# Hybrid retention and attention layer: p.v in fp32 in the two column halves of TensorE, row maxima of two heads in its two row halves

## The chip, the cores and the metric

The kernel runs on one core of a Trainium2 chip. Its time is the device time of one execution in microseconds; the figure for the kernel before is the median of three runs. The profile is of one execution, so every duration below is of that one.

TensorE is called PE in the views, VectorE DVE, ScalarE ACT and GpSimd POOL.

## What is computed

One layer, applied to two sequences with the same weights: a sequence of 1024 tokens (the prompt, names ending in `p`) and one of 512 tokens (the sample, names ending in `s`). Only the attention half of the layer is touched:

```python
def blocked_gqa(q, k, v):            # 8 query heads, 2 key/value heads, head size 64
    ...
    def one_block(qi):               # 128 queries
        sc = jnp.einsum('bqkgd,bskd->bkgqs', qi, k).astype(jnp.float32) * scale
        p = jax.nn.softmax(sc, axis=-1).astype(v.dtype)
        return jnp.einsum('bkgqs,bskd->bqkgd', p, v)
...
mixed = jnp.concatenate([ret_out * jax.nn.silu(rg), att_out * jax.nn.silu(ag)], axis=-1) @ w_out
return x + gate[:, None, :] * mixed
```

All of it is fp32. The kernel uses two ways of multiplying fp32 numbers on TensorE: operands of type fp32r, which it splits into a high and a low part to add several products, each matmul being one record in the trace; or operands left fp32, unsplit, where one matmul is two records in the trace.

## The kernel before

The sample goes first (its attention is swept at about 207 to 335 us), the prompt second (about 669 to 981 us). Attention is swept in tiles of 128 queries: four tiles for the sample, eight for the prompt (`nt`). Heads 0 to 3 share key/value head v=0, heads 4 to 7 share v=1.

Per tile, the steps and their lines are these. `nat_prep` transposes the eight heads of q, high part stacked on low part (L841), and ACT copies them to `Q1T` (L844). `nat_head`, once a head, multiplies them with the keys into a wide PSUM buffer (L854; two matmuls of 512 columns in the prompt, one in the sample), and DVE takes the negated row maximum (L856). `fill_q2`, `mid` and `mid_t` put q and the maximum side by side (POOL's copy in `pcopy`, L142; DVE's L865), transpose that (L872) and copy it to `Q2T` of 65 rows (L874), so that the score matmul of the low key part also subtracts the maximum. `st_unit`, eight times a tile in the prompt, four in the sample, makes the transposed scores of four heads against 256 keys (two matmuls L897, two L909), ACT takes the exponential (L912), ACT casts the high part `ph` (L138, in `split`), DVE subtracts for the low part `pl` (L139), and POOL adds p into an accumulator (L921, L924). `pv_unit` multiplies with v, four matmuls of 512 columns (L939, L940); v's high and low parts are side by side in the stationary operand, so the two halves of the result are added at the end (L950 on ACT, L951 on DVE). `row_sums` sums POOL's accumulator over keys with an fp32 matmul with ones, one for v=0 and one for v=1, which write to the two column halves (L958). `normalise` takes Ln and Exp of that (L963, L964), multiplies with the gate (L969) and with o (L970). `out_step` multiplies the finished tile with the output weights (`mm3`, L148 to L150, tile name `py`), 48 matmuls of 512 columns a tile. They are the work that fills the spaces of the next tile.

The order is written out in rounds, one round a unit (`per_` is nt + 1 rounds a tile); in each round the steps stand by a priority number, and a scheduler then places the instructions:

```python
at_round(hb + u, 1, lambda t=t, h=u * hp + h, n=n: nat_head(t, h, ...))
at_round(b + u, 3, lambda t=t, u=u: st_unit(t, u))
at_round(b + u + 1, 4, lambda t=t, u=u: pv_unit(t, u))
at_round(b + nt, 4.5, lambda t=t: row_sums(t))
```

`hb` is one tile ahead of `b`, so the maxima of the next tile are made while the scores of this one are. PSUM has eight banks, shared by `wide` buffers of two banks and `bank` buffers of one: two wide and four single in the sample's attention, three and two in the prompt's.

## Time and profile before

| | |
|---|---|
| time, median of 3 runs (lowest, highest) | 988.04 us (985.65, 988.46) |
| the profiled execution: span | 985.3 us |
| instructions | 15952 |
| PE busy | 938.8 us, 95% of the span |
| DVE busy | 626.1 us, 64% |
| POOL busy | 507.7 us, 52% |
| ACT busy | 414.3 us, 42% |

Of the profiled execution the span is what is known: 985.3 us, 2.7 us under the median of the three runs, which are timed without a profile. Busy is the time in which an engine's records run. A matmul's record is longer than the time to the next matmul's start, since matmuls overlap; so the price of a matmul is read from one start to the next one's.

### The profile page before, as it was taken

Reading aid. Unit: us, or ns where it says so; the run is one execution under the profiler, and the core shown is the slowest. Engines: PE = TensorE matmul, PEld = TensorE weight load, DVE = VectorE, ACT = ScalarE, POOL = GpSimd, SP = SyncE. Lnnn points to the kernel's source line nnn. Section 1 sums busy time; section 2 is a strip of 40 time slices with the busy share of each in tenths; the row PEclk is TensorE's granted clock in tenths of the full one; section 3 lists DMA queues with packets and bytes.
Section 4 is the critical chain, followed back from the end, with each engine's and each line's share of the span. In section 5 each row is a group of like instructions: output and inputs, shape, how many; then the busy total and the mean of one; then the engine's idle time right before and its main releaser. Section 6 shows DMA issues by size and latency. Waiting matters only on the chain. (4 is left out here: it accounts for less than half of the span.)

```text
span 985.3 us, 15952 instructions
## 1 busy us (share of the span) xinstructions
PE 938.8 (95%) x6249; PEld 813.9 (83%) x6249; DVE 626.1 (64%) x1039; ACT 414.3 (42%) x656; POOL 507.7 (52%) x404
## 2 busy tenths in 40 slices
PE   4889998999999999999999999999979999999998
PEld 3779898987676799999999988999847776776776
DVE  2474556667886683534435243457988878978975
ACT  4252233353646652122321322241465655655562
POOL 4243544474647663122223012255899779777882
PEclk9999998999999999999999999999999999999999
DMA  9964876321911711111111112100071110111011
GB/s 274 275 191 144 269 225 218 87 78 57 382 67 44 239 50 47 41 43 44 44 35 28 26 43 70 47 7 12 1 296 68 43 44 1 44 43 45 20 43 44
DMA packets 95687, 93.02 MB, mean 94 GB/s; under 512 B 23502, under 2 KB 84858, under 8 KB 92540
## 3 DMA queue, kind: packets, MB, share of 16 engines
q1 hardware_dynamic: 92876, 77.85, 25.8%
q0 software_dynamic: 2736, 14.16, 3.6%
q8 instruction: 49, 0.80, 0.3%
q14 instruction: 26, 0.21, 0.1%
HBM read 77.30 MB, written 14.68 MB: 93 GB/s over the span
## 5 line engine op out<-in xcount | busy, mean ns | idle before, releaser
L924 POOL TENSOR_TENSOR qp<-qp,pp 128x512 f32<-128x512 f32 x96 | 159.5, 1661 | 21.3 <-ACT pp L912 15.3
L139 DVE TENSOR_TENSOR plp<-pp,php 128x1024 fp32r<-128x1024 f32 x64 | 93.6, 1464 | 19.8 <-ACT php L138 19.7
L912 ACT ACTIVATE pp<-pTp 128x1024 f32<-128x1024 f32 x64 | 65.6, 1025 | 76.8 <-PE pTp L909 40.7
L856 DVE TENSOR_REDUCE nmp<-pnp 128x1 f32<-128x1024 f32 x64 | 77.3, 1212 | 11.4 <-PE pnp L854 11.4
L138 ACT CAST php<-pp 128x1024 fp32r<-128x1024 f32 x64 | 67.2, 1051 | 16.2 <-PE pop L939 14.9
L148 PE MATMUL pvgp<-wvgp,hhp 128*128 128x256 f32 x224 | 65.1, 291 | 0.0
L148 PE MATMUL pqkp<-wqkp,hhp 128*128 128x256 f32 x224 | 64.7, 289 | 0.0
L149 PE MATMUL pvgp<-wvgp,hhp 128*128 128x256 f32 x224 | 64.4, 288 | 0.0
L150 PE MATMUL pvgp<-wvgp,hlp 128*128 128x256 f32 x224 | 63.9, 285 | 0.0
L150 PE MATMUL pqkp<-wqkp,hlp 128*128 128x256 f32 x224 | 63.7, 284 | 0.0
L149 PE MATMUL pqkp<-wqkp,hhp 128*128 128x256 f32 x224 | 63.4, 283 | 0.0
L940 PE MATMUL pop<-plp,VVp 128*128 128x512 f32 x128 | 52.1, 407 | 5.7 <-DVE plp L139 5.6
L148 PE MATMUL pyp<-wo,Mhp 128*128 128x512 f32 (+1 forms) x136 | 52.8, 389 | 1.2 <-DVE op L951 0.7
L150 PE MATMUL pyp<-wo,Mlp 128*128 128x512 f32 (+1 forms) x136 | 51.6, 382 | 0.5 <-DVE Mlp L139 0.5
L149 PE MATMUL pyp<-wo,Mhp 128*128 128x512 f32 (+1 forms) x136 | 51.9, 382 | 0.0
L639 POOL TENSOR_TENSOR sp<-rt1p,rt2p 128x512 f32<-128x512 f32 x16 | 22.5, 1405 | 56.4 <-DVE rt2p L636 56.4
L939 PE MATMUL pop<-php,VVp 128*128 128x512 f32 x128 | 51.0, 398 | 0.3 <-ACT php L138 0.3
L124 POOL TENSOR_SCALAR m_retp<-ssp 128x4 f32<-128x4 f32 x8 | 1.6, 195 | 89.6 <-DVE ssp L745 89.4
L897 PE MATMUL pTp<-Q1Tp,kkp 128*128 128x512 f32 x128 | 41.4, 404 | 3.6 <-ACT pp L912 2.9
L148 PEld LDWEIGHTS pqkp<-wqkp,hhp 128*128 128x128 f32 x224 | 43.0, 192 | 0.0
L149 PEld LDWEIGHTS pqkp<-wqkp,hhp 128*128 128x128 f32 x224 | 43.0, 192 | 0.0
L150 PEld LDWEIGHTS pqkp<-wqkp,hlp 128*128 128x128 f32 x224 | 42.9, 192 | 0.0
(465 smaller groups left out, 3120.7 us busy)
## 6 DMA issues: line engine op xcount, KB each, us to landing
wo<-wod SPq DMA_DIRECT2D x16, 1024.0 KB, 5.8
wa<-in_w_ada_dram SPq DMA_DIRECT2D x16, 512.0 KB, 6.4
wod<-woz POOLq DMA_DIRECT2D x8, 1024.0 KB, 6.0
gr<-in_w_ada_dram SPq DMA_DIRECT2D x16, 256.0 KB, 4.8
xn<-in_x_prompt_dram SPq DMA_DIRECT2D x8, 512.0 KB
xrp<-in_x_prompt_dram SPq DMA_DIRECT2D x8, 512.0 KB, 3.4
out_dram<-xrp POOLq DMA_DIRECT2D x7, 512.0 KB, 3.0
xs<-in_x_sample_dram SPq DMA_DIRECT2D x4, 512.0 KB, 6.1
```

The source lines that it names most:

```text
L138: hi_eng(hi, src)
L139: lo_eng.tensor_tensor(lo, src, hi.bitcast(F32), op=ALU.subtract)
L148: T.matmul(out, lh, rh, start=first, stop=False)
L149: T.matmul(out, lh, rl, start=False, stop=False)
L150: T.matmul(out, ll, rh, start=False, stop=last)
L639: G.tensor_tensor(qk, t1, t2, op=ALU.add)
L856: V.tensor_reduce(nm[:, h : h + 1], pn[:, :ntok], AX.X, ALU.max, negate=True)
L897: T.matmul(pT[:, i * 512 : (i + 1) * 512], kk[v][:, kb], st8[t]["Q1T"][:, hs, :].rearrange("p h q -> p (h q)"), start=True, stop=False)
L912: S.activation(p, pT, AF.Exp)
L924: G.tensor_tensor(acc, acc, p[:, i * 512 : (i + 1) * 512], op=ALU.add)
L939: T.matmul(po, lv, ph[:, c], start=(kb == 0), stop=False)
L940: T.matmul(po, lv, pl[:, c], start=False, stop=(kb == nt - 1))
```

## The change

Four things are changed.

1. p and v are multiplied in fp32. p is not split (no cast, no subtraction), v is kept as one fp32 copy. The matmul of a head group has 64 output rows, so v=0 is put into column half 0 and v=1 into column half 1 of the array, one after the other: `pv_pair`, four matmuls for 256 keys of both v, which all wait for the exponential of the second of two units. Units therefore alternate between v=0 and v=1. The result `po` is in one bank for the whole tile and is read by `normalise` directly.
2. The row maxima are taken from the high part of q and k alone, with 64 contracted rows a head. Two heads are put into the two row halves of the array: `nat_pairs`, for two units two wide buffers, each with two heads against 512 keys. In the prompt the two maxima of a head (512 keys each) are then combined by DVE.
3. The eight maxima of a tile are transposed once (a matmul of 128 columns into 8 rows), and two DVE multiplications with a part of the identity matrix spread them over rows 64 to 71 of `Q2T`; `k2` has eight rows of ones for them. Rows 0 to 63 are copied by DVE from `Q1T`. POOL's copy and the second set of transposes fall away.
4. The two row sum matmuls stand together, behind POOL's last addition, and their buffer is a wide one. The sample's attention also has three wide buffers and two single ones.

```diff
-                kv["k2"] = [kvp.tile([65, ntok], F32R, name=f"k2{tg}{v}") for v in range(2)]
-                kv["V"] = kvp.tile([P, nt, 2, 2, DH], F32R, name=f"VV{tg}")
+                kv["k2"] = [kvp.tile([72, ntok], F32R, name=f"k2{tg}{v}") for v in range(2)]
+                kv["V"] = kvp.tile([P, nt, 2, DH], F32, name=f"VV{tg}")
...
-                        for v in range(2):
-                            src = pj[:, :, P + v * DH : P + (v + 1) * DH]
-                            S.copy(VV[:, gs_, v, v, :], src)
-                            V.tensor_tensor(VV[:, gs_, v, 1 - v, :], src, VV[:, gs_, v, v, :].bitcast(F32), op=ALU.subtract)
+                        S.copy(VV[:, gs_, :, :], pj[:, :, P : 2 * P].rearrange("p t (v d) -> p t v d", v=2))
...
-            nwide.append(2 if first else 3)
+            nwide.append(3)
...
+                Qg = Q1.rearrange("p (g h) a d -> p g (h a) d", h=2)
+                split(*((S.copy, V) if t == order[0] else (pcopy, G)), Qg[:, :, 0::3, :], Qg[:, :, 1:3, :], qv)
...
+            def fill_q2(t):
                 d = st8[t]
-                Q1T, nm = d["Q1T"], d["nm"]
-                v = h // 4
-                pn = (bank if nt == 4 else wide)(f"pn{tg}{t}{h}")
-                for n in range(ng):
-                    c = slice(n * 512, (n + 1) * 512)
-                    T.matmul(pn[:, c], Q1T[:, h, :], kk[v][:, c], start=True, stop=True)
-                with tc.issue_after(prev["mid"].ins) if "mid" in prev else ExitStack():
-                    V.tensor_reduce(nm[:, h : h + 1], pn[:, :ntok], AX.X, ALU.max, negate=True)
-
-            def fill_q2(t, v):
-                b0 = (t % 2) * 512 + v * 256
-                Q2 = st8[t]["Q2", v] = ate.tile([P, 4, 65], F32R, tag=f"Q2{v}", name=f"Q2{tg}{t}{v}", bufs=1)
-                pcopy(Q2[:, :, 0:DH], qs[t // 2][:, b0 : b0 + 256].rearrange("p (h d) -> p h d", d=DH))
-
-            def mid(t, v):
+                Q1T = d["Q1T"]
+                Q2T = d["Q2T"] = pools["q2"].tile([72, QH, P], F32R, tag="Q2T", name=f"Q2T{tg}{t}", bufs=Q2BUFS[r])
+                for i in range(2):
+                    V.tensor_copy(Q2T[0:DH, i::2, :], Q1T[i * DH : (i + 1) * DH, i::2, :])
...
+            def nat_pairs(t, units, prev):
                 d = st8[t]
-                d["mid"] = V.tensor_copy(d["Q2", v][:, :, DH], d["nm"][:, 4 * v : 4 * v + 4])
-
-            def mid_t(t, v):
+                Q1T = d["Q1T"]
+                pns = [wide(f"pn{tg}{t}{u}") for u in units]
+                with tc.high_priority():
+                    for j, u in enumerate(units):
+                        pr, n = u // ng, u % ng
+                        for i in range(2):
+                            rows = slice(i * DH, (i + 1) * DH)
+                            m = T.matmul(pns[j][:, i * 512 : (i + 1) * 512], Q1T[rows, 2 * pr + i, :],
+                                         kk[pr // 2][rows, n * 512 : (n + 1) * 512], start=True, stop=True)
+                for j, u in enumerate(units):
+                    pr, n = u // ng, u % ng
+                    out = (d["nm"] if ng == 1 else d["nmh"][:, n, :])[:, 2 * pr : 2 * pr + 2]
+                    with tc.issue_after(prev["mid"].ins) if "mid" in prev else ExitStack():
+                        V.tensor_reduce(out, pns[j].rearrange("p (i k) -> p i k", i=2), AX.X, ALU.max, negate=True)
...
+            def mid(t):
                 d = st8[t]
-                Q2 = d["Q2", v]
-                pq = wide(f"pq2{tg}{t}{v}")[:, 0:512]
-                for h in range(4):
-                    T.transpose(pq[0:65, h * P : (h + 1) * P].bitcast(F32R), Q2[:, h, :], identr)
-                q2 = d["Q2T", v] = pools["q2"].tile([65, 512], F32R, tag=f"Q2T{v}", name=f"Q2T{tg}{t}{v}", bufs=1)
-                V.tensor_copy(q2, pq[0:65, :])
+                if ng > 1:
+                    V.tensor_tensor(d["nm"], d["nmh"][:, 0, :], d["nmh"][:, 1, :], op=ALU.min)
+                pm = wide(f"pnm{tg}{t}")[0:QH, 0:P]
+                T.transpose(pm.bitcast(F32R), d["nm"], identr)
+                for v in range(2):
+                    hs = slice(4 * v, 4 * v + 4)
+                    d["mid"] = V.tensor_tensor(d["Q2T"][DH:72, hs, :], pm.unsqueeze(1).broadcast_to([QH, 4, P]),
+                                               ident[0:QH, hs].unsqueeze(2).broadcast_to([QH, 4, P]), op=ALU.mult)
...
-                split(S.copy, V, ph, pl, p)
-                d[u] = (ph, pl)
+                p = d["p", u] = pools["at"].tile([P, 1024], F32, tag="p", name=f"p{tg}{t}{u}", bufs=PBUFS[r])
+                d["exp", u] = S.activation(p, pT, AF.Exp)
...
+            def pv_pair(t, kp):
                 d = st8[t]
-                v, kp = u // (nt // 2), u % (nt // 2)
-                ph, pl = d.pop(u)
+                ps = [d.pop(("p", 2 * kp + v)) for v in range(2)]
                 if kp == 0:
-                    d["po"] = bank(f"po{tg}{t}{v}")
-                if u == 0:
-                    d["o"] = pools["q2"].tile([P, 512], F32, tag="o", name=f"o{tg}{t}", bufs=3 if first else 1)
-                po, o = d["po"], d["o"]
-                for i in range(2):
-                    kb = 2 * kp + i
-                    c = slice(i * 512, (i + 1) * 512)
-                    lv = VV[:, kb, v, :, :].rearrange("p a d -> p (a d)")
-                    T.matmul(po, lv, ph[:, c], start=(kb == 0), stop=False)
-                    T.matmul(po, lv, pl[:, c], start=False, stop=(kb == nt - 1))
-                if t in pesum:
-                    if u == 0:
-                        d["L"] = bank(f"pL{tg}{t}")
-                    for i, z in enumerate((ph, pl)):
-                        for j in range(2):
-                            T.matmul(d["L"], vones[v], z[:, j * 512 : (j + 1) * 512],
-                                     start=(u == 0 and i + j == 0), stop=(u == nt - 1 and i + j == 2))
-                if kp == nt // 2 - 1:
-                    mn = slice(v * DH, (v + 1) * DH)
-                    S.copy(o[mn, :], po[(1 - v) * DH : (2 - v) * DH, :])
-                    V.tensor_tensor(o[mn, :], po[mn, :], o[mn, :], op=ALU.add)
+                    d["po"] = bank(f"po{tg}{t}")
+                with tc.high_priority():
+                  for i in range(2):
+                    for v in range(2):
+                        m = T.matmul(d["po"][v * DH : (v + 1) * DH, :], VV[:, 2 * kp + i, v, :], ps[v][:, i * 512 : (i + 1) * 512],
+                                     start=(kp + i == 0), stop=(2 * kp + i == nt - 1))
+                        if v == 0:
+                            tc.add_manual_dep(m.ins, d["exp", 2 * kp + 1].ins.name, SYNC, reason="both column halves at once")
 
             def row_sums(t):
-                if t in pesum:
-                    return
-                pl = st8[t]["L"] = bank(f"pL{tg}{t}") if nt == 4 else wide(f"pL{tg}{t}")[:, 0:512]
+                d = st8[t]
+                pl = d["L"] = wide(f"pL{tg}{t}")[:, 0:512]
                 for v in range(2):
-                    T.matmul(pl[v * DH : (v + 1) * DH, :], ones, qs[tps[0]][:, v * 512 : (v + 1) * 512], start=True, stop=True)
+                    m = T.matmul(pl[v * DH : (v + 1) * DH, :], ones, qs[tps[0]][:, v * 512 : (v + 1) * 512], start=True, stop=True)
+                    if v == 0:
+                        tc.add_manual_dep(m.ins, d["sum", 1].ins.name, SYNC, reason="both halves at once")
...
+                lg = d["o"] = pools["q2"].tile([P, 512], F32, tag="o", name=f"o{tg}{t}", bufs=3 if first else 1)
                 with tc.issue_after(acts["ln"].ins):
...
-                V.tensor_tensor(o, o, pl, op=ALU.mult)
+                    jc = slice(jj * 256, (jj + 1) * 256)
+                    V.tensor_tensor(lg[:, jc].rearrange("p (j q) -> p j q", j=2), pl[:, jc].rearrange("p (j q) -> p j q", j=2),
+                                    gv, op=ALU.mult)
+                V.tensor_tensor(lg, po, lg, op=ALU.mult)
...
+                at_round(hb + per_ - 2 if n == 0 else b - 2, 7.5, lambda t=t: fill_q2(t))
+                at_round(hb + per_ - 1 if n == 0 else b - 1, 7, lambda t=t: mid(t))
                 for u in range(nt):
-                    for h in range(hp):
+                    if u % 2 == 0:
                         at_round(hb + u, 1,
-                                 lambda t=t, h=u * hp + h, n=n: nat_head(t, h, st8[order[0]] if n == 1 else {}))
+                                 lambda t=t, u=u, n=n: nat_pairs(t, (u, u + 1), st8[order[0]] if n == 1 else {}))
                     at_round(b + u, 3, lambda t=t, u=u: st_unit(t, u))
-                    at_round(b + u + 1, 4, lambda t=t, u=u: pv_unit(t, u))
+                    if u % 2:
+                        at_round(b + u + 1, 4, lambda t=t, u=u: pv_pair(t, u // 2))
```

On PE at the border of two tiles of the prompt (where one tile's row sums and the next tile's first scores stand) the kernel before has these rows; `pLp` is the row sums' buffer, `pnp` a maximum's, `pTp` a score's, `pop` p.v's, `pq1p` that of q's transposes:

```order
L841 MATMUL pq1p_9151<-identr,Q1p_9148 128x128 x3
L150 MATMUL pyp_9079<-wo_8052,Mlp_8890 128x512
L939 MATMUL pop_9065<-php_9114,VVp 128x512 [waits Activation_49]
L958 MATMUL pLp_9144<-qp_7145,zo 64x512 [waits Pool_49]
L940 MATMUL pop_9065<-plp_9115,VVp 128x512 [waits DVE_49]
L939 MATMUL pop_9065<-php_9114,VVp 128x512
L940 MATMUL pop_9065<-plp_9115,VVp 128x512
L854 MATMUL pnp_9174<-kkp_6773,Q1Tp_9160 128x512 [waits Activation_49]
L854 MATMUL pnp_9174<-kkp_6773,Q1Tp_9160 128x512
L897 MATMUL pTp_9187<-Q1Tp_8881,kkp_6773 128x512 [waits PE_49]
L897 MATMUL pTp_9187<-Q1Tp_8881,kkp_6773 128x512
L909 MATMUL pTp_9187<-Q2Tp_9063,k2p_6775 128x512 x2
```

After the change the same place reads as follows (line numbers are those of the changed kernel: L940 the row sums, L876 the transposed maxima, L840 q's transposes, L863 the maxima, L901 and L912 the scores):

```order
L940 MATMUL pLp_8166<-qp_6926,zo 64x512 [waits PE_49,Pool_49]
L940 MATMUL pLp_8166<-qp_6926,zo 64x512
L876 MATMUL pnmp_8170<-identr,nmp_7973 8x128 [waits PE_49]
L840 MATMUL pq1p_8177<-identr,Q1p_8174 128x128 [waits PE_49]
L840 MATMUL pq1p_8177<-identr,Q1p_8174 128x128 x7
L863 MATMUL pnp_8202<-kkp_6566,Q1Tp_8186 128x512 [waits DVE_49,Activation_49]
L863 MATMUL pnp_8202<-kkp_6566,Q1Tp_8186 128x512
L863 MATMUL pnp_8203<-kkp_6566,Q1Tp_8186 128x512 [waits PE_49]
L863 MATMUL pnp_8203<-kkp_6566,Q1Tp_8186 128x512
L901 MATMUL pTp_8219<-Q1Tp_7971,kkp_6566 128x512 [waits DVE_49,Activation_49]
L901 MATMUL pTp_8219<-Q1Tp_7971,kkp_6566 128x512
L912 MATMUL pTp_8219<-Q2Tp_8147,k2p_6568 128x512 x2
```

The two row sums now stand in a row behind POOL, q's transposes have moved behind them, and nothing of `py` or of p.v stands between the row sums and the next tile's scores.

On PE in the middle of a tile the kernel before has p.v in fours, in the full array:

```order
L150 MATMUL pyp_9079<-wo_8052,Mlp_8890 128x512
L940 MATMUL pop_9065<-plp_9053,VVp 128x512 [waits DVE_49]
L939 MATMUL pop_9065<-php_9052,VVp 128x512
L940 MATMUL pop_9065<-plp_9053,VVp 128x512
L939 MATMUL pop_9065<-php_9090,VVp 128x512 [waits Activation_49]
L148 MATMUL pyp_9079<-wo_8052,Mhp_8889 128x512
```

After it, four matmuls with 64 output rows stand behind one wait for ACT:

```order
L151 MATMUL pyp_8118<-wo_7766,Mlp_7982 128x512
L149 MATMUL pyp_8118<-wo_7766,Mhp_7981 128x512
L150 MATMUL pyp_8118<-wo_7766,Mhp_7981 128x512
L151 MATMUL pyp_8118<-wo_7766,Mlp_7982 128x512
L931 MATMUL pop_8049<-pp_8127,VVp 64x512 [waits Activation_49]
L931 MATMUL pop_8049<-pp_8143,VVp 64x512
L931 MATMUL pop_8049<-pp_8127,VVp 64x512
L931 MATMUL pop_8049<-pp_8143,VVp 64x512
L149 MATMUL pyp_8229<-wo_7765,Mhp_8196 128x512 [waits DVE_49]
```

The number of matmuls for a unit of 256 keys and four heads goes from four to two, and their four stand together.

On ACT at the same border the kernel before has:

```order
L138 CAST php_9114<-pp_9112 128x1024 [waits PE_49,Activation_49]
L138 CAST Mhp_9447<-mTp 128x512 [waits PE_49]
L844 CAST Q1Tp_9160<-pq1p_9151 128x1024 [waits PE_49]
L963 ACTIVATE pLp_9144<-pLp_9144 128x512 [waits PE_49]
L950 COPY op_8944<-pop_9065 64x512 [waits PE_49]
L964 ACTIVATE pLp_9144<-pLp_9144 128x512 [waits Activation_49]
L912 ACTIVATE pp_9192<-pTp_9187 128x1024 [waits DVE_49,PE_49,Pool_49]
L138 CAST php_9194<-pp_9192 128x1024 [waits Activation_49]
```

After the change (L949 and L950 are Ln and Exp of the row sums, L843 the copy of `Q1T`, L915 the exponential of the scores):

```order
L915 ACTIVATE pp_8143<-pTp_8138 128x1024 [waits PE_49,Pool_49]
L139 CAST Mhp_8411<-mTp 128x512 [waits DVE_49,PE_49]
L949 ACTIVATE pLp_8166<-pLp_8166 128x512 [waits DVE_49,PE_49,Activation_49]
L843 CAST Q1Tp_8186<-pq1p_8177 128x1024 [waits PE_49]
L950 ACTIVATE pLp_8166<-pLp_8166 128x512 [waits Activation_49]
L915 ACTIVATE pp_8224<-pTp_8219 128x1024 [waits PE_49,Pool_49]
L139 CAST Mhp_8196<-op_8190 128x512 [waits DVE_49]
L915 ACTIVATE pp_8238<-pTp_8233 128x1024 [waits PE_49,Pool_49]
```

The casts `php` are gone, and the copy of `Q1T` has moved from ahead of Ln to between Ln and Exp.

## Rows read from the trace of the kernel before

**Rows 1.** The page, part 1: busy time of an engine, its share of the span, instructions.
```profile
PE 938.8 (95%) x6249; PEld 813.9 (83%) x6249; DVE 626.1 (64%) x1039; ACT 414.3 (42%) x656; POOL 507.7 (52%) x404
```

**Rows 2.** Windows of the two attention stages: length, busy us of each engine, granted clock.
```profile
247.00:335.00 88.00, 86.06 (x376) 62.98 (x375) 63.80 (x84) 50.34 (x70) 52.17 (x48) 1.00 0.47 175
696.00:981.00 285.00, 272.00 (x1213) 203.88 (x1212) 235.55 (x251) 163.67 (x184) 228.49 (x148) 0.99 0.15 58
```

**Rows 3.** Source line L958: minimum/median/maximum ns, first and last start.
```profile
L958 PE MATMUL pLp<-qp,zo x32: 592/642/1112, 720.5 to 969.1; 128*64 128x512 f32 x32
```

**Rows 4.** Timeline of PE: start us, length us, line, operation, names, how many.
```profile
748.11 0.41 PE L872 MATMUL pq2p<-identr,Q2p 128*65 128x128 f32 x4
748.35 0.44 PE L940 MATMUL pop<-plp,VVp 128*128 128x512 f32 x1
748.63 0.39 PE L939 MATMUL pop<-php,VVp 128*128 128x512 f32 x1
748.86 0.40 PE L940 MATMUL pop<-plp,VVp 128*128 128x512 f32 x1
```

**Rows 5.** Timeline of PE around one L958.
```profile
765.83 0.40 PE L940 MATMUL pop<-plp,VVp 128*128 128x512 f32 x1
766.15 1.07 PE L958 MATMUL pLp<-qp,zo 128*64 128x512 f32 x2
767.15 0.50 PE L149 MATMUL pyp<-wo,Mhp 128*128 128x512 f32 x1
767.49 0.39 PE L150 MATMUL pyp<-wo,Mlp 128*128 128x512 f32 x1
```

**Rows 6.** Timeline of PE, ACT and DVE around the last two L958.
```profile
968.60 1.08 PE L958 MATMUL pLp<-qp,zo 128*64 128x512 f32 x4
...
969.61 0.50 PE L148 MATMUL pyp<-wo,Mhp 128*128 128x512 f32 x1
...
969.75 0.58 ACT L963 ACTIVATE pLp<-pLp 128x512 f32<-128x512 f32 x1 [4.52 <-PE pLp L958]
...
970.36 0.58 ACT L964 ACTIVATE pLp<-pLp 128x512 f32<-128x512 f32 x1
...
970.98 0.90 DVE L969 TENSOR_TENSOR pLp<-pLp,gp 128x256 f32<-128x256 f32 x2 [2.92 <-ACT pLp L964]
```

**Rows 7.** Waits of PE, 696 to 981: engine, line, releaser: us, times, longest.
```profile
PE pop L940 <- DVE plp L139: 5.6, 6, 1.2
PE pTp L897 <- ACT pp L912: 2.9, 3, 2.1
PE pLp L958 <- POOL qp L924: 1.5, 1, 1.5
```

**Rows 8.** Lines of 696 to 981: us busy, mean ns | idle before, and its releasers.
```profile
L924 POOL TENSOR_TENSOR qp<-qp,pp 128x512 f32<-128x512 f32 x96 | 159.5, 1661 | 21.3 <-ACT pp L912 15.3 <-POOL qp L924 0.4
L139 DVE TENSOR_TENSOR plp<-pp,php 128x1024 fp32r<-128x1024 f32 x64 | 93.6, 1464 | 19.8 <-ACT php L138 19.7
L856 DVE TENSOR_REDUCE nmp<-pnp 128x1 f32<-128x1024 f32 x56 | 67.8, 1212 | 8.9 <-PE pnp L854 8.9
...
L912 ACT ACTIVATE pp<-pTp 128x1024 f32<-128x1024 f32 x64 | 65.6, 1025 | 76.8 <-PE pTp L909 40.7 <-DVE plp L139 14.3 <-POOL qp L924 9.0
```

**Rows 9.** Timeline of PE and ACT around the q transposes of one tile.
```profile
758.25 0.79 PE L841 MATMUL pq1p<-identr,Q1p 128*128 128x128 f32 x8
...
758.88 0.46 PE L148 MATMUL pyp<-wo,Mhp 128*128 128x512 f32 x1
...
759.24 1.01 ACT L844 CAST Q1Tp<-pq1p 128x1024 fp32r<-128x1024 f32 x1
```

**Rows 10.** Timeline of POOL: an addition while DVE does nothing beside it.
```profile
764.27 1.29 POOL L924 TENSOR_TENSOR qp<-qp,pp 128x512 f32<-128x512 f32 x1
```

**Rows 11.** Windows: a stretch ahead of a lowered clock, and the stretch itself.
```profile
727.00:733.80 6.80, 4.42 (x16) 2.37 (x14) 6.72 (x6) 4.30 (x6) 6.80 (x6) 1.00 0.44 128
733.80:737.20 3.40, 3.38 (x6) 1.49 (x7) 2.52 (x3) 2.14 (x3) 3.40 (x3) 0.50 1.02 429
```

More of the change, by code (lines that the diff above doesn't have):

```diff
@@ L39 @@
 KPOST = (1, 1)
-PESUM = (0, 0)
+PBUFS = (6, 8)
+Q2BUFS = (1, 2)
 EPS = 1e-6
@@ L114, in hybrid_layer_kernel @@
     V.memset(mhalf, -0.5)
-    zo = cst.tile([P, 4, DH], F32R, name="zo")
-    for i in range(4):
+    zo = cst.tile([P, 3, DH], F32R, name="zo")
+    for i in range(3):
         V.tensor_scalar(out=zo[:, i, :], in0=ident[:, 0:DH], scalar1=0.0, scalar2=float(i == 2), op0=ALU.mult, op1=ALU.add)
@@ L119, in hybrid_layer_kernel @@
     ones = zo[:, 2, :].bitcast(F32)
-    vones = [zo[:, 2 - v : 4 - v, :].rearrange("p i d -> p (i d)") for v in range(2)]
     def rsqrt(pl, ss, n, mul, add, name):
@@ new lines, in nat_prep @@
+                S.copy(Q1T.rearrange("p h q -> p (h q)"), pq)
+                d["nm"] = ate.tile([P, QH], F32R, tag="nm", name=f"nm{tg}{t}")
+                d["nmh"] = ate.tile([P, ng, QH], F32, tag="nmh", name=f"nmh{tg}{t}") if ng > 1 else None
+            def fill_q2(t):
+                d = st8[t]
+                Q1T = d["Q1T"]
+                Q2T = d["Q2T"] = pools["q2"].tile([72, QH, P], F32R, tag="Q2T", name=f"Q2T{tg}{t}", bufs=Q2BUFS[r])
+                for i in range(2):
+                    V.tensor_copy(Q2T[0:DH, i::2, :], Q1T[i * DH : (i + 1) * DH, i::2, :])
@@ L908, in st_unit @@
                     kb = slice((2 * kp + i) * P, (2 * kp + i + 1) * P)
-                    T.matmul(pT[:, i * 512 : (i + 1) * 512], k2[v][:, kb], d["Q2T", v],
+                    T.matmul(pT[:, i * 512 : (i + 1) * 512], k2[v][:, kb], d["Q2T"][:, v * 4 : v * 4 + 4, :].rearrange("p h q -> p (h q)"),
                              start=False, stop=True)
-                p = pools["at"].tile([P, 1024], F32, tag="p", name=f"p{tg}{t}{u}")
-                S.activation(p, pT, AF.Exp)
-                ph = pools["at"].tile([P, 1024], F32R, tag="ph", name=f"ph{tg}{t}{u}", bufs=3 if first else 2)
```

53 lines of the change are left out of this document (18 added, 35 removed).

## The prediction

> **What bounds the kernel now.** I read the page first: PE is busy for 95% of the span [rows 1]. Then the two attention stages by windows: PE 86.06 us of 88 in the sample's, 272.00 of 285 in the prompt's, with DVE at 235.55 and POOL at 228.49 [rows 2]. So PE sets the time, and a change is worth what it does to PE's work plus what it does to PE's waits. A busy record is longer than what a matmul costs, so I price matmuls by starts. One of 512 columns in fp32r: 748.63 to 748.86, 0.23 us, called a slot here; four transposes of q2: 748.11 to 748.35, 0.24 [rows 4]; eight of q: 758.25 to 758.88, 0.63 [rows 9].
>
> One fp32 matmul into a column half: the matmul before it starts at 765.83, L958 at 766.15, the next two slots at 767.15 and 767.49 [rows 5]. From 765.83 to 767.49 are 1.66 us; two ordinary slots in it are 0.46, so the excursion into half the array costs 1.20. It is two records of 512 columns; the 1.00 us between starts is a bit over four slots (0.92). I book 0.92 as work and 0.28 as the price of going into a half and back. Two of them that stand together, one in each half (x4 records), take from 968.60 to 969.61: 1.01 us [rows 6], the same as one. So column halves run side by side, and a pair costs what a single one costs.
>
> A prompt tile: the first L958 of the eight tiles starts at 720.5 [rows 3], the last at 968.60, seven tiles on: 35.4 us a tile. Its PE work is 128 slots (16 maxima, 32 scores, 32 p.v, 48 of the output projection), 29.4 us, two excursions of 1.20, 0.63 and twice 0.24: 33.0. The rest, 2.4 us a tile or 19 us over eight, are waits and lowered clock; the views name part of them: p.v for DVE's low part 5.6, scores for the exponential 2.9, a row sum for POOL 1.5 [rows 7].
>
> **PE's work after the change.** I count by excursions of 0.28.
>
> - p.v: in the prompt 32 groups of four fp32 matmuls, two pairs each, 2 x 0.92 + 0.28 = 2.12 against 8 slots, 1.84. That is +0.28 each, +9.0; in the sample 8 groups, +2.2. The fp32 products thus save nothing on PE: they only take the split away from ACT and DVE.
> - Maxima: if row halves run side by side as column halves do, 16 slots of a prompt tile become 8: -1.84 a tile, -14.7. The sequence enters row halves 41 times in the prompt: +11.5. Together -3.2. In the sample four slots fewer a tile, -3.7, and 14 entries, +3.9: +0.2. No row of before has a matmul in row halves. The bounds of one entry are 0 (the array may not need to empty between row halves and whole) and 0.28 (as for a column half, with its own passes); I take 0.28, the nearest row being that of a change between halves and whole [rows 5].
> - Row sums: in the prompt seven of the eight tiles had two single excursions and now have one pair: -8.4. In the sample four: -4.8.
> - q2's transposes, 0.48 a tile, give way to one of the maxima, about 0.25 with its change of shape: -1.8 and -0.9.
> - In 13 places of the order a row group is followed by a column group without whole-array work between, which saves half an excursion: -1.8, all counted in the prompt.
>
> Prompt: 9.0 - 3.2 - 8.4 - 1.8 - 1.8 = -6.2. Sample: 2.2 + 0.2 - 4.8 - 0.9 = -3.3. PE's work falls by 9.5 us.
>
> The Trainium skill ("TensorEngine Tiling (Array Packing)", Tiling Modes) says that changing the tiling mode drains TensorE, which speaks against a change that goes from 44 such changes to about 200. The 0.28 us of [rows 5] agrees for column halves; no run here shows it yet for row halves.
>
> **ACT, DVE and POOL.** A tile loses eight casts on ACT, eight subtractions of 1464 ns on DVE (11.7 us), POOL's copies of q2 [rows 8]. DVE falls from about 29 to some 17 us in a tile of 35. None of it is on the path by itself; it is worth the 5.6 us of p.v's waits, and faster additions on POOL (1.29 us where DVE is idle beside it [rows 10], 1661 ns on average [rows 8]).
>
> **PE's waits after the change.** Here I lose more than PE's work gives back, and the place is the border of two tiles. Call E the moment at which the row sum pair has left PE (969.61 in [rows 6]). Before the change p.v, output projection and scores stand around it, so Ln, Exp and gate run beside work. In the new order nothing of that stands between the row sums and the next scores. From E: the maxima's transpose 0.25 and q's 0.63 keep PE till 0.88. ACT's copy of q starts when they are through (758.25 + 0.79 is 0.79 after their start [rows 9], so 1.1) and takes 1.01 [rows 9]: 2.1. The first maxima wait for it. Their two units take 4 x 0.23, halved side by side, plus an excursion, 0.74: 2.9. Exp stands behind that copy on ACT: it runs 2.1 to 2.7 (0.58 [rows 6]), then DVE's two gate multiplications 0.90 [rows 6], to 3.6. The first scores take the wide buffer that the row sums hold, so they wait till 3.6. PE has had 1.6 us of work in 3.6: 2.0 idle. The second unit's scores then wait for the maximum of the first (1212 ns on DVE [rows 8], 3.6 to 4.8), the next maxima for the second (6.0), and the first p.v group for the second exponential (1025 ns each [rows 8], about 7.0): 0.8 more. That is 2.8 at a border. Five of the seven read so; behind the first tile 12 projection matmuls stand there, 0.5; ahead of the last tile some stand there, 2.0. The borders sum to 16.5.
>
> At a tile's end the last p.v group waits for the eighth exponential (1.4 with nothing between, 0 behind 12 projection matmuls), and the row sums, which now wait for POOL's last addition, for four of 1.29 (2.2 with nothing between, 0.9 behind 12 matmuls ahead of p.v, 0 with more on both sides). By the order the first two tiles have 3.6 each, three have 0.5, two have 0.9, the last is covered by the retention's steps: 10.5. In the middle of a tile I take 4 over the whole sweep, about what scores waiting for the exponential cost now [rows 7] and a little for pairs. Sum 31, against 19: +12. The sample, with four short tiles whose borders have projection work, gets +1.
>
> **The clock.** One stretch of before has a lowered clock: granted 0.50, the lower of the two levels (1.2 GHz), from 733.8 to 737.2, after PE had been busy 4.42 of 6.80 us [rows 11], the last of it a wait of 1.5 for POOL [rows 7]. Its six records are one row sum and four slots, 2.1 at full clock, and took 3.4: 1.3, about 1.5 with the edge. The two stops of 3.6 at a tile's end followed by a border are like it, and one border more may be: three times 1.5, +4.5.
>
> **Sum.** -9.5 + 12 + 1 + 4.5 = +8. Against the span 985.3 that is 993.3; the three runs have a median of 988.04, 2.7 above the span, so 996.0.
>
> **Rivals.** *Row halves are nearly free* (R1). Nothing in the trace has them. For it: the transposes of q2 are a change of shape too (65 columns), and the slot behind them is 0.28 [rows 4], 0.05 late, so not every change costs 0.28. Without the 55 entries' 0.28 the time falls by 15.4: 981. It decides below 0.13 us an entry (8/55 taken from 0.28), where the time equals before. *The waits are no worse* (R2): the scheduler's order shows 2.8 at a border only if DVE's multiplication comes at 3.6; DVE and ACT have some 40% less work, and if Exp, gate and maxima come about 2 us earlier, or lowered clocks do not come, +13 falls away: 983, faster. It decides at 8 of the 17.5 us. Both R1 and R2: 968. *The clock falls at most borders* (R3): twelve instead of three, 9 x 1.5 more: 1010. For it speaks the stretch ahead of [rows 11], against it that most stops here are shorter than that stretch's 2.4. *Row halves are not side by side* (R4): 64 prompt slots and 16 of the sample come back, 80 x 0.23 = 18.4: 1014. The column pair of [rows 6] speaks against it. The Trainium skill ("TensorE: Matmul & The Clock Gate", Part 3) measures packed row tiles as running at once, which by itself would exclude R4.
>
> **Numbers.** A measurement here tells a change from 0.3%, 3 us. The forecast, 988 to 1006, has 0.38 (0.08 of it within 3 us of before, 0.30 slower); R1 0.20 (0.17 faster, 0.03 same); R2 0.18 (0.13, 0.05); both 0.06, faster; R3 0.12 and R4 0.06, slower. Faster 0.36, same 0.16, slower 0.48. Cases of both signs hold the chance, so the range goes from 974, between R1 and both, to 1012, over R3: it leaves out both (0.06), most of R4, and the ends of the others.
>
> **What would show it.** PE's idle time at the prompt's borders near 2.8 us, released by DVE's gate multiplication and the maxima; a pair of maxima starting 0.3 us late and a slot lost behind it; four p.v matmuls in 1.9 to 2.1 us; row sums in one pair of 1.0; DVE near 150 us in the window of the prompt. Wrong it is if maxima cost no entry (0.46 for four matmuls with no gap at either side), if the scores after the row sums start before E + 2.9, or if the granted clock stays at 1.00 through the borders.

## The result, and the profile after

The changed kernel takes 1000.27 us (median of 4 runs, 998.48 to 1001.2), the kernel before 987.83 beside it: a ratio of 1.0126, with an interval of 1.0109 to 1.0142. It is slower, and 4 us above the forecast of 996.

The profiled execution has a span of 998.2 us. The page's row of busy time on PE, which answers to [rows 1]:

```profile
PE 931.7 (93%) x6165; PEld 750.0 (75%) x6165; DVE 511.2 (51%) x914; ACT 317.7 (32%) x546; POOL 428.8 (43%) x380
```

The windows of the two attention stages, which answer to [rows 2] (the prompt's from its first scores to the end of its sweep):

```profile
247.00:335.00 88.00, 82.59 (x375) 54.08 (x372) 41.88 (x59) 35.02 (x52) 41.78 (x45) 1.00 0.49 184
693.00:994.00 301.00, 272.12 (x1160) 157.74 (x1161) 149.79 (x178) 88.24 (x104) 164.57 (x135) 0.96 0.14 55
```

Up to the prompt's first scores the changed kernel is ahead: they start at 693.3 us, before at 695.9, so 2.6 were gained (booked: 2.3), 1.9 of it between the sample's first scores and the prompt's. From there to the end it takes 304.9 us, before 289.3: the prompt lost 15.6 (booked: 10.3). DVE, ACT and POOL did get light: DVE is busy 149.79 of 301 us there, where it had 235.55 of 285. PE is busy as long as before (272.12 and 272.00 us) and stands 28.9 us instead of 13.0, so the loss is not work that PE was given but time in which it stood; and part of the busy time, as the clock below shows, it ran slowly.

PE's waits of the prompt, which answer to [rows 7]:

```profile
PE pLp L940 <- POOL qp L921: 8.7, 4, 3.8
PE pnp L863 <- ACT Q1Tp L843: 5.5, 5, 1.1
PE pop L931 <- ACT pp L915: 4.4, 8, 1.2
PE pyp L149 <- DVE xrp L1007: 3.3, 3, 1.1
PE pTp L901 <- DVE op L955: 3.2, 5, 0.6
```

POOL's additions did get shorter, as the lines of the same stage show, the first of which answers to the first of [rows 8]; the maxima's reduction on DVE stayed as it was:

```profile
L921 POOL TENSOR_TENSOR qp<-qp,pp 128x512 f32<-128x512 f32 x96 | 124.8, 1325 | 67.5 <-ACT pp L915 66.5
L869 DVE TENSOR_REDUCE nmhp<-pnp 128x2 f32<-128x1024 f32 x56 | 67.1, 1219 | 63.7 <-PE pnp L863 63.7
```

One border of two tiles, all engines (L940 the row sums, L876 the transposed maxima, L840 q's transposes, L949 and L950 Ln and Exp, L843 the copy of Q1T, L863 the maxima, L955 the gate, L901 the scores):

```profile
805.19 1.08 PE L940 MATMUL pLp<-qp,zo 128*64 128x512 f32 x4
...
806.20 0.22 PE L876 MATMUL pnmp<-identr,nmp 128*8 128x128 f32 x1
...
806.26 0.84 PE L840 MATMUL pq1p<-identr,Q1p 128*128 128x128 f32 x8
806.37 0.58 ACT L949 ACTIVATE pLp<-pLp 128x512 f32<-128x512 f32 x1 [6.75 <-issue]
...
807.14 1.01 ACT L843 CAST Q1Tp<-pq1p 128x1024 fp32r<-128x1024 f32 x1 [0.20 <-PE pq1p L840]
...
808.05 0.59 ACT L950 ACTIVATE pLp<-pLp 128x512 f32<-128x512 f32 x1
...
808.21 0.73 PE L863 MATMUL pnp<-kkp,Q1Tp 64*128 64x512 f32 x4 [1.10 <-ACT Q1Tp L843]
808.68 0.76 DVE L955 TENSOR_TENSOR op<-pLp,gp 128x256 f32<-128x256 f32 x2 [0.94 <-ACT pLp L950]
...
809.58 0.70 PE L901 MATMUL pTp<-Q1Tp,kkp 128*128 128x512 f32 x2 [0.64 <-DVE op L955]
...
813.00 0.50 PE L149 MATMUL pyp<-wo,Mhp 128*128 128x512 f32 x1 [0.52 <-ACT Mhp L139]
```

This is the border that was walked ahead of the run. With E at 806.20, the first maxima start at E + 2.0 (booked 2.1), idle 1.1; Exp ends at E + 2.4 (2.7), the gate at E + 3.2 (3.6), and the first scores start at E + 3.4, after 0.64 of idle. The second scores do not wait for a maximum as booked, but at this border, alone of the five, 0.5 is lost a little later at the projection, which waits for ACT's cast of o.

A lone pair of maxima in row halves (no second pair behind it) and a p.v group behind it (PE's timeline; the first two rows are ordinary slots):

```profile
792.33 0.39 PE L150 MATMUL pyp<-wo,Mhp 128*128 128x512 f32 x1
792.55 0.39 PE L151 MATMUL pyp<-wo,Mlp 128*128 128x512 f32 x1
792.87 0.51 PE L863 MATMUL pnp<-kkp,Q1Tp 64*128 64x512 f32 x2
793.30 0.50 PE L149 MATMUL pyp<-wo,Mhp 128*128 128x512 f32 x1
793.64 0.40 PE L150 MATMUL pyp<-wo,Mhp 128*128 128x512 f32 x1
793.97 1.94 PE L931 MATMUL pop<-pp,VVp 128*64 128x512 f32 x8
795.84 0.73 PE L901 MATMUL pTp<-Q1Tp,kkp 128*128 128x512 f32 x2
796.41 0.64 PE L912 MATMUL pTp<-Q2Tp,k2p 72*128 72x512 f32 x2
```

The two matmuls of the pair take 0.51 together, where two in the whole array take 0.73 (the first scores of the border above, without their wait, 0.70): the row halves run side by side. But the pair starts 0.32 after a slot of 0.23, the matmul behind it 0.43 later, and that one's successor 0.34 later. With 0.09, 0.43 and 0.11 the pair takes 0.63 to 0.65, where two slots take 0.46; the whole trip is 0.40 more than the 0.23 of the pair's columns. The p.v group takes 0.10 + 1.87 + 0.11 = 2.08 (booked 2.12), against 1.84. Two pairs in a row are better off:

```profile
731.23 0.40 PE L151 MATMUL pyp<-wo,Mlp 128*128 128x512 f32 x1
731.56 0.73 PE L863 MATMUL pnp<-kkp,Q1Tp 64*128 64x512 f32 x4
732.22 0.73 PE L901 MATMUL pTp<-Q1Tp,kkp 128*128 128x512 f32 x2
732.79 0.40 PE L912 MATMUL pTp<-Q2Tp,k2p 72*128 72x512 f32 x1
```

0.10 ahead, 0.66 and 0.11 behind make 0.87, against 0.92 for four slots.

The Trainium skill ("TensorEngine Tiling (Array Packing)", Tiling Modes) says without a price that a change of the tiling mode drains TensorE; the trace agrees, at 0.4 us for a trip into row halves and 0.24 for one into column halves.

Last, the clock. Four stretches of the prompt stand at the lower level (granted 0.50, 1.2 GHz), where [rows 11] showed one of 3.4:

```profile
723.50:730.50 7.00, 6.31 (x21) 4.03 (x22) 5.05 (x8) 3.37 (x6) 2.54 (x3) 0.51 1.01 411
771.40:778.00 6.60, 6.58 (x18) 2.43 (x16) 4.78 (x6) 2.56 (x3) 2.54 (x2) 0.50 0.01 2
846.30:853.00 6.70, 6.68 (x19) 2.89 (x18) 5.20 (x6) 2.55 (x3) 2.54 (x2) 0.50 0.00 0
921.30:924.60 3.30, 3.22 (x8) 2.41 (x8) 2.79 (x3) 1.15 (x2) 0.04 (x1) 0.52 0.57 230
```

They are 23.6 us long, and PE is busy nearly throughout, so at full clock that work would have taken about half: up to 11.8 lost, against 1.7 before. The first begins while PE waits 3.8 for POOL, ahead of the first border's row sums; the other three start 4 to 5 us behind the start of the row sums of the second, fourth and sixth border. Behind the third, fifth and seventh there is none.

### The profile page after: what moved, and what is told of

Read it like the earlier page. It is cut to its first block, busy times and chain, and to the rows that moved or that the text cites. A ratio compares the mean times of both kernels' runs of the same rounds, so it can differ in the third digit from the quotient of the medians.

```text
span 998.2 us, 15453 instructions
## 1 busy us (share of the span) xinstructions
PE 931.7 (93%) x6165; PEld 750.0 (75%) x6165; DVE 511.2 (51%) x914; ACT 317.7 (32%) x546; POOL 428.8 (43%) x380
## 5 line engine op out<-in xcount | busy, mean ns | idle before, releaser
L921 POOL TENSOR_TENSOR qp<-qp,pp 128x512 f32<-128x512 f32 x96 | 124.8, 1325 | 67.5 <-ACT pp L915 66.5
L869 DVE TENSOR_REDUCE nmhp<-pnp 128x2 f32<-128x1024 f32 x64 | 76.5, 1218 | 63.7 <-PE pnp L863 63.7
L915 ACT ACTIVATE pp<-pTp 128x1024 f32<-128x1024 f32 x64 | 64.1, 1025 | 140.9 <-PE pTp L912 136.0
L931 PE MATMUL pop<-pp,VVp 128*64 128x512 f32 x256 | 65.0, 631 | 4.4 <-ACT pp L915 4.4
L901 PE MATMUL pTp<-Q1Tp,kkp 128*128 128x512 f32 x128 | 45.5, 435 | 4.6 <-DVE op L955 3.2
L901 PEld LDWEIGHTS pTp<-Q1Tp,kkp 128*128 128x128 f32 x128 | 22.3, 196 | 29.8 <-issue 18.2
L912 PE MATMUL pTp<-Q2Tp,k2p 72*128 72x512 f32 x128 | 43.2, 420 | 0.2 <-DVE Q2Tp L879 0.2
L931 PEld LDWEIGHTS pop<-pp,VVp 128*64 128x64 f32 x256 | 16.1, 141 | 36.1 <-issue 25.5
L149 PEld LDWEIGHTS pvgp<-wvgp,hhp 128*128 128x128 f32 x224 | 42.9, 191 | 0.0
```

What stands on the lines that cost most here:

```text
L149: T.matmul(out, lh, rh, start=first, stop=False)
L869: V.tensor_reduce(out, pns[j].rearrange("p (i k) -> p i k", i=2), AX.X, ALU.max, negate=True)
L901: T.matmul(pT[:, i * 512 : (i + 1) * 512], kk[v][:, kb], st8[t]["Q1T"][:, hs, :].rearrange("p h q -> p (h q)"), start=True, stop=False)
L912: T.matmul(pT[:, i * 512 : (i + 1) * 512], k2[v][:, kb], d["Q2T"][:, v * 4 : v * 4 + 4, :].rearrange("p h q -> p (h q)"), start=False, sto ...
L915: d["exp", u] = S.activation(p, pT, AF.Exp)
L921: d["sum", v] = G.tensor_tensor(acc, acc, p[:, i * 512 : (i + 1) * 512], op=ALU.add)
```

## The experiments

All ratios are against the kernel before, run on the same chip. The changed kernel stands at 1.0126.

**Row halves undone.** Each head again in the whole array, in the same buffers and places.

```diff
-  m = T.matmul(pns[j][:, i * 512 : (i + 1) * 512], Q1T[rows, 2 * pr + i, :],
-               kk[pr // 2][rows, n * 512 : (n + 1) * 512], start=True, stop=True)
+  m = T.matmul(pns[j][:, i * 512 : (i + 1) * 512], Q1T[:, 2 * pr + i, :],
+               kk[pr // 2][:, n * 512 : (n + 1) * 512], start=True, stop=True)
```

> The row halves alone are undone: each head's maximum is again made with all 128 contracted rows, two matmuls of 512 columns one after the other, in the same buffers and at the same places. Theory A (changes of mode cost more than pairing saves): in the trace after the change a lone pair of maxima takes 0.43 us and delays what stands ahead and behind by 0.11 each, 0.65, against 0.46 for two slots; two pairs together about 0.98 against 0.92. With 18 lone and 23 double entries in the prompt and 14 in the sample that is 5 to 8 us back: 993 to 995, with the lowered clock as it is. Rival (pairing pays in the stage, since the maxima come earlier): 1002 or more.

991.89 us, ratio 1.0035 (1.0011 to 1.0059): 8 us back, as theory A said, and a little more. But not for its reason. The profiled execution is the fastest of ten: they go from 988.2 us at a mean clock of 0.996 (this one) to 996.0 at 0.987, so what follows shows the run at its best. Windows of it: its one stretch of lowered clock in the sweep, the time behind the row sums of its second border, and one whole tile.

```profile
719.50:726.80 7.30, 6.19 (x22) 3.91 (x23) 4.92 (x8) 3.80 (x6) 2.96 (x3) 0.53 1.01 411
764.00:767.30 3.30, 2.13 (x8) 1.35 (x8) 2.37 (x5) 1.43 (x2) 1.89 (x2) 1.00 0.02 5
798.00:834.00 36.00, 33.24 (x142) 20.35 (x141) 18.18 (x22) 11.13 (x13) 20.64 (x17) 1.00 0.09 29
```

The last two of these places in the changed kernel, and behind them the time behind its fifth border, of which more below:

```profile
768.10:771.40 3.30, 1.62 (x8) 0.97 (x8) 2.37 (x4) 1.48 (x2) 1.89 (x2) 0.98 0.00 0
805.00:841.00 36.00, 32.84 (x143) 18.59 (x141) 21.72 (x22) 11.12 (x13) 20.09 (x17) 1.00 0.15 49
882.50:885.80 3.30, 1.70 (x8) 0.97 (x8) 2.37 (x5) 1.40 (x2) 1.85 (x2) 1.00 0.54 159
```

A tile at full clock is a little longer with row halves than without: from one pair of row sums to the next, the changed kernel's two tiles without a stretch take 36.2 and 36.5, and this run's 36.0 to 36.1. The trips cost somewhat more than the pairing saves. The larger part of what is gone is three stretches of lowered clock: tiles of 39.1, 39.0 and 37.1 us are 36.0 to 36.1 in this run, some 6 us more than the trips explain. Behind the row sums PE is busy 2.13 of 3.3 us, where with row halves it was 1.62: the maxima take half the time, but the waits around them end when ACT and DVE are done, so PE only stands longer. That alone does not decide it: at 882.5 the changed kernel has 1.70 of 3.3 and no stretch follows.

**A filler at the border.** Six matmuls without a reader, into the buffer of the first maxima and ahead of them.

```diff
+FILL = (0, 6)
...
+  def filler(ps, k, behind):
+      for i in range(0 if first else FILL[k]):
+          with tc.issue_after(behind.ins):
+              behind = T.matmul(ps[:, 0:512], kk[i % 2][:, 0:P], kk[i % 2][:, 0:512], start=True, stop=True)
...
+  if units[0] == 0 and t != order[0]:
+      filler(pns[0], 1, st8[t]["turned"])
```

> Six matmuls that nobody reads (512 columns each, 1.4 us) are put between q's transposes and the first maxima at each border of the prompt's tiles but the first, where PE waits 1.06 us for ACT's copy of Q1T. Work is added, 9.7 us in all, and nothing taken away. Theory B (the emptied border lowers the clock afterwards, about 3.3 us for each of the four stretches at 0.50): some of the stretches go and the time stays within 4 us of 1000 or falls, although 9.7 us were added and only some 7 of it lie in waits. Theory A (clock not tied to the border): the stretches stay and the time rises to 1003 to 1006.

999.03, ratio 1.0106 (1.0060 to 1.0152): with 9.7 us more work on PE no slower, as theory B said. In its profile the borders from the third on have no stretch left, and a tile is 35.7 us; a new stretch of 3 us stands in the first tile (700 to 704), and one each is left at the first and the second border. In the order the projection's matmuls also moved ahead of the last p.v group, so this run alone does not prove it.

```profile
810.00:846.00 36.00, 33.77 (x149) 19.77 (x150) 22.64 (x23) 11.25 (x13) 20.90 (x18) 1.00 0.10 35
```

**Row sums one round later**, behind the next tile's first maxima (prompt only).

```diff
-  at_round(b + nt, 4.5, lambda t=t: row_sums(t))
+  lt = 0 if first or t == final else 1
+  at_round(b + nt + lt, 2.5 if lt else 4.5, lambda t=t: row_sums(t))
```

Ln, Exp, gate and the cast of the result move by `lt` too.

> In the prompt the row sums, Ln, Exp and the gate of a tile are put one round later, behind the next tile's first maxima, so that neither PE's wait for POOL's last addition nor the wait of the first scores for the row sums' wide buffer stands at the border. Theory B (the loss is the border and the clock behind it): two to four stretches of lowered clock go (3.3 each) and about 2 us a border: 975 to 988. Theory A (the loss is the changes of mode): their number stays, 996 to 1000.

995.12, ratio 1.0067 (1.0042 to 1.0092). The total lies between the two readings, just under theory A's. Theory A's reason does not fit: the tiles without a stretch fall from 36.2 and 36.5 to 34.9 and 34.3, and the prompt takes 296.4 us, 8.5 less than the changed kernel's 304.9. But four stretches of lowered clock stand in the prompt as before, against theory B. In this profile the prompt's first scores start 4 us later (697.4); 3 of them lie ahead of the sample's first scores, which the edit does not touch, and 1 in the sample, where one more stretch stands (254 to 257).

**p.v undone**, to split fp32r in the whole array, with the units in the order of before; row halves, mask and paired sums stay.

```diff
-  p = d["p", u] = pools["at"].tile([P, 1024], F32, tag="p", ...)
+  split(S.copy, V, ph, pl, p)
...
-  at_round(b + u + 1, 4, lambda t=t, u=u: pv_pair(t, u // 2))
+  at_round(b + u + 1, 4, lambda t=t, u=u: pv_unit(t, u))
```

> Only p.v is undone: p and v split into high and low parts again, four fp32r matmuls a unit in the whole array, units in the order of before, cast on ACT and subtraction on DVE back; the maxima in row halves, their one transpose and the paired row sums stay. If p.v in fp32 is what costs (its groups wait for the second exponential and leave the border empty): the time falls below that of before, to 978 to 988, since the row sums' pairing and q2's transposes stay saved. If the maxima in row halves are what costs: 994 or more.

1021.07, ratio 1.0334 (1.0294 to 1.0373): slower still. That is on the rival's side (994 or more), but 21 us above the changed kernel, which neither reading foresaw. So p.v in fp32 is not what costs.

**Both undone.** 

> Both parts are undone: p.v is in split fp32r as in the run of 1021 us, and the maxima are made with 128 rows as in the run of 992 us; what stays is the one transpose of the maxima, the mask, the paired row sums and the order of units. With the four times the two parts can be told apart. If the loss of the row halves is only what PE's changes of mode take (5 to 8 us), this run gives 1013 to 1016. If the row halves also bring PE into the lower clock (in the run of 1021 us five stretches in the prompt, three in the sample; one in the run of 992 us), the stretches go with them and it gives 985 to 998.

1015.95, ratio 1.0279 (1.0256 to 1.0303): beside the run before it the row halves cost 5 us, and 28 us above the kernel before are neither part's. Half of them lie ahead of the prompt: from the sample's first scores to the prompt's first it takes 476.6 us (477.9 in the run before it), where the kernel before takes 462.1 and the changed one 460.2. These runs have two single PSUM banks in the sample, where before had four, and one buffer fewer for the low part of p, so the sample says nothing on p.v. In the prompt alone: 289.3 before, 309.5 with neither, 313.2 with row halves, 296.3 with fp32 p.v, 304.9 with both. p.v in fp32, with its order of units, saves 8 to 13 us there, the row halves cost 4 to 9, and what the runs keep of the change (among it one transpose and mask for all heads, maxima two units at a time, sums in one pair at the end) costs 20 with the old p.v.

**Both: whole-array maxima and late sums.** The first and the third edit together.

> Row halves undone and the prompt's row sums one round later, both at once. If the two gains add (8 and 5 us): 987, level with before. If the lowered clock that was left in the run with late sums (four stretches) came from the row halves: it goes too, and 978 to 984, faster than before. If the two gains are the same gain twice (the same stretches of lowered clock): 992.

982.69 us, ratio 0.9944 (0.9926 to 0.9961): faster than both kernels. The gains add: 1.0126 - 0.0091 - 0.0059 would be 0.9976, and the little that it is better lies within the intervals. Of the four stretches that the late sums alone had left, those at the second and third border are gone, so the second reading holds in part. Tiles are 34.4 us. PE no longer waits for the copy of Q1T, and for the gate once, 0.2; what is left stands in its timeline (L140 DVE's split of the retention half, L1007 the last addition that frees the projection's bank):

```profile
791.37 1.28 DVE L879 TENSOR_TENSOR Q2Tp<-pnmp,identr 8x512 fp32r<-8x512 f32 x2
...
792.14 1.19 PE L863 MATMUL pnp<-kkp,Q1Tp 128*128 128x512 f32 x4
...
792.68 1.45 DVE L140 TENSOR_TENSOR Mlp<-mTp,Mhp 128x512 fp32r<-128x512 f32 x1
794.05 0.68 DVE L1007 TENSOR_TENSOR xrp<-pyp,xrp 128x512 f32<-128x512 f32 x1
...
794.78 0.50 PE L149 MATMUL pyp<-wo,Mhp 128*128 128x512 f32 x1 [1.44 <-DVE xrp L1007]
...
797.71 1.08 PE L940 MATMUL pLp<-qp,zo 128*64 128x512 f32 x4
...
798.72 0.74 PE L901 MATMUL pTp<-Q1Tp,kkp 128*128 128x512 f32 x2
```

**q's transposes two rounds earlier**, with whole-array maxima.

```diff
-  at_round(hb - (4 if n == 1 else 1), 8, lambda t=t: nat_prep(t))
+  at_round(hb - (4 if n == 1 else 3), 8, lambda t=t: nat_prep(t))
```

> Row halves undone, and q's transposes for the tile after next two rounds earlier, so that ACT's copy of Q1T no longer stands between Ln and Exp at the border. In the run with the row halves undone alone PE waited 5.5 us for that copy, 1.1 at each of five borders, and 0.9 for the gate. If these waits are what the border costs: 5 to 6 less than 992, 986. If PE then waits for POOL's last additions in their place (the order puts the projection's twelve matmuls ahead of the last p.v group): 990 to 993.

999.3, ratio 1.0108 (1.0079 to 1.0137): 7 us worse than without it, which neither reading had. The wait for Q1T is gone, but PE waits nearly as long at the same place for DVE (4.6, 5 times), 3.0 for maxima that DVE makes, and a stretch of 7 us at the lower clock has come in the sample (252 to 259). Between the sample's first scores and the prompt's it takes 6.2 us longer than in the profile with whole-array maxima alone (the edit moves the sample's transposes too); the prompt takes 1.9 longer there, so it gains nothing either.

**Trips without their work**: two matmuls of 64 columns in row halves ahead of each unit's whole-array maxima.

```diff
+  T.matmul(pns[j][:, i * 512 : i * 512 + 64], Q1T[rows, 2 * pr + i, :],
+           kk[pr // 2][rows, n * 512 : n * 512 + 64], start=True, stop=True)
```

> The kernel with the row halves undone (992 us), with the change of mode put back without its work: ahead of the two whole-array matmuls of each unit of maxima stand two of 64 columns in the two row halves, whose result is overwritten. 80 more trips into row halves and back (64 in the prompt, 16 in the sample), each 0.03 us of columns. If a trip costs what the rows around lone pairs show (0.11 ahead, 0.11 behind, 0.2 to run empty), the time rises by 25 to 33 us, to 1017 to 1025, 3 us a tile of the prompt and more if the clock falls with it. If the row halves' loss was only that of the lowered clock and a trip is nearly free: 992 to 998.

1009.51, ratio 1.0223 (1.0193 to 1.0253): 17.6 us more than with whole-array maxima alone, for 80 trips: between the two. The price of one is as in the changed kernel (PE's timeline):

```profile
836.39 0.39 PE L151 MATMUL pyp<-wo,Mlp 128*128 128x512 f32 x1
836.71 0.30 PE L863 MATMUL pnp<-kkp,Q1Tp 64*128 64x64 f32 x2
836.93 0.74 PE L866 MATMUL pnp<-kkp,Q1Tp 128*128 128x512 f32 x2
837.60 0.30 PE L863 MATMUL pnp<-kkp,Q1Tp 64*128 64x64 f32 x2
837.83 0.74 PE L866 MATMUL pnp<-kkp,Q1Tp 128*128 128x512 f32 x2
```

From one trip's start to the next one's, 836.71 to 837.60, are 0.89 us, and the two slots between are 0.46: a trip costs 0.43, 0.03 of it columns. At borders it falls into waits, so a tile is 38.0 us, 1.9 longer and not 3.4. And the clock did not fall with it: no stretch stands between 735 and 1004, and the four executions have a mean clock of 0.992 to 0.994. Changes of mode alone do not bring it here.

**Neither, with late sums.** 

> Split fp32r p.v and whole-array maxima, as in the run of 1016 us, and the prompt's row sums one round later. If the row sums at the border are a cost whatever p.v is: 8 us less, 1006 to 1010. If with p.v in single units the border was already covered by p.v and projection, so that the sums cost nothing there: 1013 to 1019.

1005.33, ratio 1.0174 (1.0146 to 1.0202): 10.6 us less than the run without late sums, so the sums at the border cost with either p.v; in the prompt 298.9 us instead of 309.5, so half of the 20 us above is theirs.

**Retention half a tile earlier**, on the fastest kernel.

```diff
+  if not first and n and t != final:
+      at_round(b + GR, 9.2, lambda t=t: gate_ret(t))
```

> The fastest kernel so far (whole-array maxima, late row sums, 982.7 us), with the retention half of the next projection's operand cast and subtracted one tile earlier, so that DVE's subtraction of 1.45 us no longer stands between the end of one projection half and the start of the next, where PE waits 1.4 at five borders for the tile's last addition. If that subtraction is what is late: 975 to 979. If DVE's order leaves the last addition where it is, behind the same subtraction for the tile after: 981 to 984.

984.68, ratio 0.9961 (0.9944 to 0.9977), no gain: DVE's order keeps a subtraction of 1.45, now the one for the tile after, ahead of the addition, and PE waits 7.5 in five places for it as before.

**Whole-array maxima only at the border, and only inside** (there the condition is `units[0] > 0`).

```diff
-  rows = slice(i * DH, (i + 1) * DH)
+  rows = slice(0, P) if units[0] == 0 else slice(i * DH, (i + 1) * DH)
```

> The changed kernel with whole-array maxima for the first two units of each tile only, the four matmuls that stand at the border behind the row sums; the other six units of a prompt tile stay in row halves. If the row halves lose because they leave PE less to do at the border, and the clock falls behind it: most of the gain of the run with all of them undone, 992 to 995, no stretch of lowered clock behind the third to sixth border. If they lose by their trips wherever they stand: one part in four of it, 997 to 999.

998.18, ratio 1.0103 (1.0074 to 1.0132). The time is in the rival's reading (trips wherever they stand). The clock did as foreseen by the first, but in the profiled execution, the fastest of four (mean clock 0.994, the others 0.986 to 0.989): tiles of 36.5 us without a stretch behind any border from the third on (one of 3 us stands in the last tile instead).

```profile
802.70:839.20 36.50, 33.42 (x142) 18.96 (x141) 18.20 (x22) 11.14 (x13) 20.59 (x17) 1.00 0.09 30
```

> The opposite: row halves for the first two units only, at the border, and whole-array maxima for all others. If the border decides: the stretches behind borders stay, 997 to 1001. If the trips decide wherever they stand: three parts in four of the gain, 993 to 995.

996.38, ratio 1.0087 (1.0057 to 1.0117), between the two readings. Here four of the five tiles from the second border on have a stretch of some 3 us, mean clock 0.95; the one from the fourth border to the fifth has none and is about 1 us shorter. Three of the five:

```profile
766.10:803.20 37.10, 34.00 (x143) 21.10 (x143) 18.18 (x22) 11.14 (x13) 20.67 (x17) 0.95 0.01 2
839.80:875.90 36.10, 32.87 (x143) 20.00 (x143) 18.42 (x23) 11.14 (x13) 20.65 (x17) 1.00 0.02 7
875.90:913.20 37.30, 33.99 (x142) 21.19 (x141) 18.19 (x22) 11.13 (x13) 20.68 (x17) 0.95 0.08 28
```

In the profiles the two parts add to the whole: the prompt is 301.2 and 300.1 us, 3.7 and 4.8 below 304.9, together 8.5; with both it was 8.6. The timed runs agree within their intervals (2 and 4 us of 8). So the row halves' loss is neither at the border alone nor inside the tiles alone.

## Why the prediction held, by its steps

*PE's work.* p.v was booked at +0.28 a group and is +0.24. The row sums' pair is 1.01 as booked. The maxima were mis-sized twice: a trip into row halves costs 0.40, not the 0.28 taken from the column halves, and in the trace the prompt enters them 46 times, not 41: 29 lone pairs, 16 times two pairs, once three (which take 1.08 where six slots take 1.38). So at full clock they are 29 x 0.19 - 16 x 0.05 - 0.3 = +4.4 instead of -3.2. That settles R1 (nearly free) and R4 (not side by side) against both: side by side, and not free.

*The waits.* The order at the border was as walked, with less idle: 1.1 + 0.64 + 0.5 = 2.2 us of the 2.8 booked at the border shown, 1.7 to 2.1 at the four others like it, 9.8 over all borders instead of 16.5. The first tile's end went as booked (3.6), PE waiting 3.8 for POOL. The tile ends together took 15.1 instead of 10.5: 8.7 for POOL, 3.1 of the 4.4 for the exponential, and 3.3 that were not seen ahead, at the ends of three tiles, where the twelve projection matmuls that were meant as cover wait 1.1 for DVE's last addition to free their bank. So the 31 booked for the sweep were near the measured 28.9 because two errors met. The 19 booked for the kernel before was a remainder, and too high: it stands 13.0 there [rows 2], and its lowered clock adds 1.7 at most. Idle time thus grew by 15.9, where 12 were booked, and R2 (waits no worse) fell.

*The clock* was too small a term: three stretches of 1.5 were booked, 4.5, and four came, three of them 6.6 to 7 us long, up to 10 us more than before. In number that is near the booking, in size between it and R3 (twelve of 1.5). These 6 us, the maxima's 7.6 and the waits' 4 are far more than the 4 between forecast and result; p.v gave 1.3 back, and for the remainder no row accounts. So the direction and one main cause, the waits that the new order makes, were foreseen; that the sum came within 4 us is in part luck.

*What the runs show of the cause.* Of the prompt's 15.6 us, whole-array maxima give back 8.6, late sums 8.5, and the two together 16.7 (288.2 us): with both, nothing of the loss is left. (The timed medians give 8.4, 5.2 and 17.6.) For the late sums the mechanism is shown: the wait for POOL and for the wide buffer leaves the border, and tiles fall from 36.1 to 34.4. For the row halves it is shown only in part: at full clock a tile is 0.2 to 0.5 us longer with them, which the trips' prices explain; in the profiles the rest, some 6 us, is stretches of lowered clock, which follow borders in which PE stands longer, and most of which go when the border is filled or made in the whole array. Why a stretch follows one border and not the next with the same rows stays open, and so does why it differs between executions of one kernel. Of the 4.8 us of the inside units the trips of the prompt's sweep are about 4 (24 lone pairs, nine times two: 24 x 0.19 - 9 x 0.05). That p.v in fp32 helps here, by 8 to 13 us, is shown for the prompt, in this structure.

## What to carry to other kernels

Pairing matmuls in halves of the array pays only from a group size that earns the trip: here 0.4 us a trip into row halves, so a lone pair of 512 columns loses 0.19 and two pairs gain 0.05. Count the trips in the order that ran, not the matmuls. When an edit makes engines lighter and joins work in groups that wait together, walk the places where such groups meet: idle time there is paid twice if the clock falls behind it, and moving one pair of row sums by a round was worth 5 us, where undoing the row halves gave 8.

## What had not been expected of the hardware

PE at the lower clock for 23.6 us of the prompt although it was 90% busy over the sweep (272.12 of 301.00); 80 added trips into row halves, at 0.4 us each, brought no further stretch (mean clock 0.994), while half a us less of work behind the row sums (1.62 against 2.13 of 3.3) went with three, though not at every border. And one kernel's executions differ by it: with whole-array maxima the mean clock lies between 0.987 and 0.996, and the time between 996.0 and 988.2 us.
